# Layer 0 of a two-layer decoder trunk: two of four output-projection groups by seven products

## The chip, the cores and the metric

The kernel runs on one core of a Trainium2 chip. TensorE (PE in the profile) multiplies matrices, with its weight loads shown apart (PEld); VectorE is DVE, ScalarE is ACT, GpSimd is POOL, and SyncE (SP) issues most DMAs. The metric is the device time of one launch in microseconds; lower is better.

## The reference

Two layers (D = 2048, 512 tokens, batch 1), each a modulated mixer with residual. Cut to what matters:

```python
for l in range(DEPTH):                                   # DEPTH = 2
    mod = c_act @ w_mod[l] + b_mod[l]                    # 2048 -> 3 x 2048
    shift, scale, gate = jnp.split(mod, 3, axis=-1)
    h = rmsnorm(x, norm_gain[l]) * (1.0 + scale[:, None, :]) + shift[:, None, :]
    proj = h @ w_in[l]                                   # 2048 -> 7504
    ...  # sparse softmax attention (8 heads) -> y_a, chunked retention (8 heads) -> y_b,
    ...  # each times its own SiLU gate
    y = jnp.concatenate([y_a, y_b], axis=-1) @ w_out[l]  # 2048 -> 2048
    x = x + gate[:, None, :] * y
```

## The kernel before, in words

Everything is held transposed: features on the 128 partitions, 512 tokens along the free axis, so x is 16 tiles of 128x512 float32 (k = 0 to 15). To keep float32 accuracy, each operand of a large product is split into a high part (rounded to fp32r, made on ACT) and a low part (the rest, made on DVE); a product is three matmuls, high-high, high-low and low-high.

The work is one stream of groups. A group is a product with 512 columns of a weight, cut into chunks of two feature tiles, eight chunks in all. A plain chunk takes 2 x 4 x 3 = 24 matmuls with 512 moving columns (`chunk_mm`, L390 to L392, or L396 to L398 where the weights move). Groups of a layer in order: S (keys, values, index), QI or Q3, VB, four QK, two QA, two GA, two GB (all of `w_in`), then four of `w_out`. Attention, retention and other work between products are Python generators (tasks) from which `fill` issues some before each chunk.

`step(i)` issues one chunk: `ahead` loads weights up to four chunks ahead (tile wf, on SP's queue) and splits them two ahead (wh on ACT, wl on DVE; each has three buffers), then the group's `pre`, then modulation, then tasks, then the chunk's matmuls. The order on each engine's queue is set when the program is built, by a scheduler, and is not always that in which the program issues; POOL's order is that of the program.

**Modulation.** `c_act @ w_mod` runs on DVE: `mod_rest` walks the list REST of 64 row tiles (gate of layer 0, shift and scale of layer 1, gate of layer 1), loads each as two halves of 128x1024 (512 KB each, tile mw, two buffers of tag mw, on SP) and `mod_add` (L408) reduces each half against the broadcast vector cb (L417). A tiny POOL copy (L416) holds each reduction behind the newest wl. `MODN` says how many halves a chunk of a group takes, as a running fraction; the last two chunks of layer 0 take none (MX0 = 2). Layer 0 needs the first 96 halves: with the last, `mod_end` (L421) adds the bias and layer 1's shift and scale are ready.

**Output projection.** Layer 0: four plain groups named OUT. `put_y` splits the gated y into high and low (kept in arena tiles HP) while GB's second group runs. `evac_out` (L1461) multiplies by the gate and adds x, which `pre_out` loaded (xr); the new x tile stays in arena tile A(k), its square goes into ssq (`add_sq`), and it is stored to xs for layer 1's residual. The last two chunks are run as two halves of 256 tokens (`out_halves`) so that layer 1's norm (prs, prb) and first h (`make_hh`, L795) start early.

Layer 1: four groups named O7 by seven products. A chunk is a 2x2 block scheme: weights of 256x512 as four blocks of 256 columns and tokens in two halves of 256, seven block products instead of eight. `seven_hi` and `seven_lo` split three blocks of the weights as they are and make four sums (wsum) and split these (ws, in tiles of tag mw, or in pairs of generic tiles); `put_seven` makes and splits four sums of y. Each of the seven products is 2 x 3 matmuls with 256 moving columns: 42 a chunk (L1354 to L1356), into seven PSUM tiles held over the group. `seven_out` combines them on DVE; `seven_put` scales by the gate, POOL adds x from memory in a DMA (`accum_op`, L1398) and POOL stores the result (L1399); the fourth quarter goes by `seven_fin` with x loaded to a tile xr, stored from SP.

Generic tiles (128x512) come from one pool of 28 buffers; PSUM has eight banks under two tags, px (tasks) and pj (groups).

Of the kernel before, what the change touches and what calls it, by code (L numbers as in the profile page):

```python
# [21 lines left out]
P = 128  # L22
# [24 lines left out]
MODN = [{"QA": 0.5, "GA": 1.0, "GB": 1.5, "OUT": 1.65}, {"QK": 0.5, "GA": 1.0}]  # L47
# [89 lines left out]
def hybrid_trunk(ctx, tc, xt, positions, wmod, w_in, w_out, cst_d, dec_d, out):  # L137
# [35 lines left out]
    def f(a):  # L173
        return a.bitcast(F32)
# [79 lines left out]
    st = {"dma": 0, "hi": 0, "split": 0, "i": 0, "mod": 0.0}  # L254
# [11 lines left out]
    def seven_hi(i):  # L266

        if "sum" not in seven:
            seven["sum"] = sm("wsum", D, tag="cb")
        w, s = wf[i], seven["sum"][:, i % 2 * 1024:(i % 2 + 1) * 1024]  # L270
        h = ring.tile([P, 1024], F32R, name="wh", tag="wh")
        act(h[:, :3 * QC], w[:, QC:], AF.Copy)
        tt(s[:, :2 * QC].rearrange("p (b c) -> p b c", c=QC), w[:, :QC].unsqueeze(1).to_broadcast([P, 2, QC]),
           w[:, 2 * QC:].rearrange("p (b c) -> p b c", c=QC), op=OP.subtract)
        tt(s[:, 2 * QC:3 * QC], w[:, 2 * QC:3 * QC], s[:, QC:2 * QC], op=OP.subtract)
        tt(s[:, 3 * QC:], w[:, QC:2 * QC], s[:, 2 * QC:3 * QC], op=OP.subtract)
        if i % 3 < 2:
            t = gen_mw("ws", F32R)
            pieces = [(t[:, :1024], t[:, 1024:], slice(0, 1024))]
        else:  # L280
            pieces = [(G("wsh", F32R), G("wsl", F32R), slice(n * T, (n + 1) * T)) for n in range(2)]
        for sh, _, c in pieces:
            act(sh, s[:, c], AF.Copy)
        whl[i] = h, s, pieces

    def seven_lo(i):
        h, s, pieces = whl[i]
        lo = ring.tile([P, 1024], F32R, name="wl", tag="wl")
        tt(lo[:, :3 * QC], wf.pop(i)[:, QC:], f(h[:, :3 * QC]), op=OP.subtract)
        for sh, sl, c in pieces:  # L290
            tt(sl, s[:, c], f(sh), op=OP.subtract)

        def part(q):
            if q < 3:
                return h[:, q * QC:(q + 1) * QC], lo[:, q * QC:(q + 1) * QC]
            c0 = (q - 3) * QC
            sh, sl, c = next(p for p in pieces if p[2].start <= c0 < p[2].stop)
            o = c0 - c.start
            return sh[:, o:o + QC], sl[:, o:o + QC]
        whl[i] = h, lo, part  # L300
# [50 lines left out]
    def step(budget=3.0, modn=2):  # L351
        i = st["i"]
        st["i"] += 1
        g, ch = stream[i]
        first, last = ch == 0, ch == g.nch - 1
        ahead(i + 5, i + 3)
        if g.pre:
            g.pre(ch)
        st["mod"] += modn
        if whl:  # L360
            state["gate"] = f(whl[max(whl)][1][:, :1])
        while st["mod"] >= 1.0:
            st["mod"] -= 1.0
            next(modgen, None)
# [121 lines left out]


# [32 lines left out]
    def put_seven(p, y0, y1):  # L520
# [24 lines left out]
        put(("T2", "T4"), t24, eh, 0, el, 0)  # L545
        YT[p] = names
# [397 lines left out]
    def layer(l):  # L944
# [386 lines left out]
        def post_seven(ch):  # L1331
            for p in (ch - 1,) if 0 < ch < 7 else (6, 7) if ch == 7 else ():
                put_seven(p, Y.pop(2 * p), Y.pop(2 * p + 1))
# [42 lines left out]
        outv = out.rearrange("(k p) t -> k p t", p=P)  # L1376

        def pre_seven(g):
            def pre(ch):
                if ch == g.nch - 3:  # L1380
# [10 lines left out]
        def seven_put(g, i, t, v):  # L1391
# [7 lines left out]
            (dma if g.end else nc.gpsimd.dma_start)(out=xs_of(outv, g, i, t), in_=halves(v))  # L1399

# [6 lines left out]
        def seven_fin(g, prod, m):  # L1407
# [4 lines left out]
            dma(outv[k][:, t * QC:(t + 1) * QC], r[:, c])  # L1412

# [34 lines left out]
        def pre_out(g):  # L1448
            def pre(ch):
                if ch == 0:  # L1450
                    for n in range(4):
                        t = G("xr")
                        dma(t, xs_d[l][4 * g + n])
                        xr[4 * g + n] = t
            return pre

        def evac_out(g):
            def ev(n, ps):
                k = 4 * g + n
                t = A(k, "xn") if first else G("xo")  # L1460
                stt(t, ps, mod_col(l, 2, k), xr.pop(k), op0=OP.mult, op1=OP.add)  # L1461
                if first:
                    X[k] = t
                    if k == 0:
                        ss["t"] = G("ssq")
                    if k < KT - 4:
                        add_sq(ss["t"], t, k)
                    if k == KT - 5:
                        act(sm("dummy", 1), ss["t"][:, :1], AF.Sqrt)
                    if k < KT - 4:  # L1470
                        dma(xs_d[1][k], t)
                else:
                    dma(out[k * P:(k + 1) * P, :], t)
            return ev

        def out_halves(i):
# [5 lines left out]
            for hf, c in enumerate(HALF):  # L1482
                q = [G("sq") for _ in range(2)]
                for n in range(4):
                    k = KT - 4 + n
                    ps = psum.tile([P, T], F32, name="po", tag=("px", "pj")[hf])[:, :nh]
# [15 lines left out]
                pss, r = PX("prs"), sm("rcol2", 2, bufs=2)  # L1502
# [6 lines left out]
                pb = PX("prb")[:, c]  # L1509
# [9 lines left out]
        S = Group(W_in, [(KA, 256), (KI, 80)], 2, "tok", 4, hact, evac_s, pre=None if first else pre_l1, name="S")  # L1519
# [55 lines left out]
        for g in range(4):  # L1575
            cols = [(QB + 256 * g, 256), (KB + 256 * g, 256)]
            if first and 4 + 2 * g < NE:
                keys = [(4 + 2 * g, 0), (5 + 2 * g, 0), (4 + 2 * g, 1), (5 + 2 * g, 1)]
                seq.append(Group(W_in, cols, 2, "t", 4, hact, joined(keys, evac_qk(g), T), name="QK",
                                 kr=(EARLY[4 + 2 * g], KT)))  # L1580
            else:
                seq.append(Group(W_in, cols, 2, "t", 4, hact, evac_qk(g), name="QK"))
        seq += [Group(W_in, [(QA + 512 * g, 512)], 2, "tok", 4, hact, evac_qa(g), name="QA") for g in range(2)]
        seq += [Group(W_in, [(GA + 512 * g, 512)], 2, "t", 4, hact, evac_g(4 * g), name="GA") for g in range(2)]
        seq += [Group(W_in, [(GB + 512 * g, 512)], 2, "t", 4, hact, evac_g(8 + 4 * g),
                      post=(post_last if first else post_seven) if g == 1 else None, name="GB") for g in range(2)]
# [58 lines left out]
```

## Time and profile before

| | us |
|---|---|
| median of 3 runs | 1850.31 |
| lowest, highest | 1849.68, 1850.46 |
| the profiled execution's own time | 1849.68 |
| its span, first to last instruction | 1847.9 |
| TensorE (PE) busy | 1821.7 |
| VectorE (DVE) busy | 1384.4 |
| ScalarE (ACT) busy | 888.0 |

The mean granted TensorE clock of the execution is 0.994 of full speed. Times in the views are microseconds from the span's start. Approximate places: layer 0's fourth QK group 416 to 469, QA 469 to 571, GA 571 to 696, GB 696 to 783, output groups 783 to 946 and their halves to 960; layer 1's second GB group 1637.6 to 1681.1 and its output groups from 1681.1 on. Rows of instructions read: line, engine, operation, tile written <- tiles read, count, busy time, mean ns of one, and idle time before it with what ended it. In rows of one tile the three numbers are the least, median and greatest ns, then first and last start.

### The profile page before, as it was taken

Reading aid. Unit: us, or ns where it says so; the run is one execution under the profiler, and the core shown is the slowest. Engines: PE = TensorE matmul, PEld = TensorE weight load, DVE = VectorE, ACT = ScalarE, POOL = GpSimd, SP = SyncE. Lnnn points to the kernel's source line nnn. Section 1 sums busy time; section 2 is a strip of 40 time slices with the busy share of each in tenths; the row PEclk is TensorE's granted clock in tenths of the full one; section 3 lists DMA queues with packets and bytes.
Section 4 is the critical chain, followed back from the end, with each engine's and each line's share of the span. In section 5 each row is a group of like instructions: output and inputs, shape, how many; then the busy total and the mean of one; then the engine's idle time right before and its main releaser. Section 6 shows DMA issues by size and latency. Waiting matters only on the chain.

```text
span 1847.9 us, 26300 instructions
## 1 busy us (share of the span) xinstructions
PE 1821.7 (99%) x9644; PEld 1562.9 (85%) x9644; DVE 1384.4 (75%) x2438; ACT 888.0 (48%) x1708; POOL 70.8 (4%) x184
## 2 busy tenths in 40 slices
PE   7999999999999999999999999999999999999998
PEld 7878888888888888888899988888888888889998
DVE  7996699787867846777776699377875686369886
ACT  7668943564546532422235542344444554245443
POOL 0001000000000000100000000000000000000111
PEclk7999999999999999999999999999999999999999
DMA  9995533333454547789864323444534354333554
GB/s 371 364 321 178 165 88 92 109 114 95 123 186 123 174 147 236 233 281 308 304 208 129 103 80 100 142 124 147 155 120 124 93 185 135 102 92 109 149 151 130
DMA packets 175762, 304.55 MB, mean 165 GB/s; under 512 B 16960, under 2 KB 92864, under 8 KB 172048
## 3 DMA queue, kind: packets, MB, share of 16 engines
q1 hardware_dynamic: 171328, 295.23, 50.5%
q0 software_dynamic: 4160, 7.41, 1.6%
q8 instruction: 76, 1.25, 0.3%
q14 instruction: 54, 0.44, 0.1%
q10 hardware_dynamic: 144, 0.22, 0.0%
HBM read 289.18 MB, written 13.63 MB: 164 GB/s over the span
## 4 chain that ended last, share of the span: by engine, by line
PE 83%; DVE 2%; ACT 2%; DMA 1%; issue 1%; SPq 0%; DVEq 0%; ACTq 0%
PE pj L390 15%; PE pj L391 15%; PE pj L392 15%; PE pj L398 6%; PE pj L397 6%; PE pj L396 6%; PE p L1356 3%; PE p L1355 3%; PE p L1354 3%; PE ptr L177 1%; PE pdot L1028 1%; DVE wl L334 1%; PE pdot L1030 1%; ACT wh L324 1%; PE plg L1250 1%
## 5 line engine op out<-in xcount | busy, mean ns | idle before, releaser
L324 ACT ACTIVATE wh<-wf 128x1024 fp32r<-128x1024 f32 (+2 forms) x277 | 284.7, 1029 | 586.9 <-PE pj L391 390.1
L334 DVE TENSOR_TENSOR wl<-wf,wh 128x1024 fp32r<-128x1024 f32 (+2 forms) x277 | 326.6, 1180 | 289.1 <-ACT wh L324 282.5
L390 PE MATMUL pj<-h,wh 128*128 128x512 f32 (+1 forms) x1280 | 488.4, 382 | 1.9 <-ACT bt L911 1.7
L391 PE MATMUL pj<-h,wh 128*128 128x512 f32 (+1 forms) x1280 | 485.9, 380 | 2.6 <-DVE h L631 2.6
L392 PE MATMUL pj<-h,wl 128*128 128x512 f32 (+1 forms) x1280 | 485.7, 379 | 0.5 <-DVE wl L334 0.5
L390 PEld LDWEIGHTS pj<-h,wh 128*128 128x128 f32 x1280 | 240.6, 188 | 44.9 <-issue 2.5
L391 PEld LDWEIGHTS pj<-h,wh 128*128 128x128 f32 x1280 | 240.6, 188 | 42.1 <-DVE h L631 3.8
L392 PEld LDWEIGHTS pj<-h,wl 128*128 128x128 f32 x1280 | 240.5, 188 | 41.4 <-DVE wl L334 1.1
L396 PE MATMUL pj<-wh,h 128*128 128x512 f32 (+1 forms) x616 | 234.6, 381 | 4.1 <-ACT h L625 3.4
L397 PE MATMUL pj<-wl,h 128*128 128x512 f32 (+1 forms) x616 | 233.6, 380 | 0.7 <-DVE wl L334 0.7
L398 PE MATMUL pj<-wh,h 128*128 128x512 f32 (+1 forms) x616 | 232.6, 380 | 0.2 <-DVE h L631 0.2
L396 PEld LDWEIGHTS pj<-wh,h 128*128 128x128 f32 x616 | 116.5, 189 | 26.7 <-ACT h L625 3.9
L397 PEld LDWEIGHTS pj<-wl,h 128*128 128x128 f32 x616 | 116.5, 189 | 20.3 <-DVE wl L334 1.1
L398 PEld LDWEIGHTS pj<-wh,h 128*128 128x128 f32 x616 | 116.2, 189 | 20.4 <-DVE h L631 0.4
L417 DVE CUSTOM_DVE_ANT_0 mw<-mw,cb 128x1024 f32<-128x1024 f32 (+1 forms) x64 | 93.0, 1453 | 7.0 <-POOL mp L416 5.6
L417 DVE CUSTOM_DVE_ANT_0 mw<-mw,cb,mp 128x1024 f32<-128x1024 f32 x68 | 88.3, 1298 | 12.4 <-POOL md L416 7.9
L392 PE MATMUL pj<-y,wl 128*128 128x512 f32 x240 | 93.4, 389 | 0.0
L391 PE MATMUL pj<-y,wh 128*128 128x512 f32 x240 | 93.4, 389 | 0.0
L390 PE MATMUL pj<-y,wh 128*128 128x512 f32 x240 | 93.4, 389 | 0.0
L1262 ACT ACTIVATE bias<-bias,mx 128x128 f32<-128x128 f32 (+1 forms) x64 | 35.9, 561 | 65.3 <-DVE mx L1261 64.6
L1036 DVE SCALAR_TENSOR_TENSOR iacc<-relu,wi,iacc 128x384 f32<-128x384 f32 (+2 forms) x96 | 55.5, 613 | 10.1 <-ACT relu L1034 7.2
L894 ACT ACTIVATE ind<-pos,pt 128x512 bf16<-128x512 f32 (+3 forms) x128 | 61.4, 553 | 0.1
(549 smaller groups left out, 3077.3 us busy)
## 6 DMA issues: line engine op xcount, KB each, us to landing
wf<-in_w_in_dram SPq DMA_DIRECT2D x155, 512.0 KB, 3.7
mw<-in_wmod_dram SPq DMA_DIRECT2D x136, 512.0 KB, 5.7
wf<-in_w_in_dram SPq DMA_DIRECT2D x136, 256.0 KB, 3.1
mw<-in_wmod_dram SPq DMA_DIRECT2D x28, 1024.0 KB, 8.6
wf<-in_w_out_dram SPq DMA_DIRECT2D x32, 512.0 KB, 5.3
wf<-in_w_out_dram SPq DMA_DIRECT2D x64, 256.0 KB, 3.5
dec<-in_decay_dram SPq DMA_DIRECT2D x32, 256.0 KB, 4.0
xT<-in_xt_dram SPq DMA_DIRECT2D x16, 256.0 KB, 5.4
```

The lines of the kernel that those rows point to most:

```text
L324: act(h[:, :n], wf[i][:, :n], AF.Copy)
L334: tt(lo[:, :n], wf.pop(i)[:, :n], f(whl[i][:, :n]), op=OP.subtract)
L390: mm(q, wh[:, o:o + P], ah, start=s0, stop=False)
L391: mm(q, wh[:, o:o + P], al, start=False, stop=False)
L392: mm(q, wl[:, o:o + P], ah, start=False, stop=s1)
L396: mm(q, ah[:, n * P:(n + 1) * P], wh[:, o:o + g.N], start=s0, stop=False)
L397: mm(q, ah[:, n * P:(n + 1) * P], wl[:, o:o + g.N], start=False, stop=False)
L398: mm(q, al[:, n * P:(n + 1) * P], wh[:, o:o + g.N], start=False, stop=s1)
L417: nc.vector.tensor_tensor_reduce(w[:, lo:hi], w[:, lo:hi], cb[:, lo:hi], scale=ng(l, k, 1) if q == 1 else 1.0, scalar=init, op0=OP.mult, o ...
L894: act(v, tab["pos"][:, :w], AF.Sign, bias=tab["pt"][:, col:col + 1], scale=-1.0)
L1036: stt(a[:, :w], r[:, :w], L["WI"][:, c0:c0 + 1], a[:, :w], op0=OP.mult, op1=OP.add)
L1354: mm(dst[m], wh[:, c], bh, start=k == 0 and (own or m == 0), stop=False)
```

## The change

In layer 0 the first two of the four output groups (NW = 2) become O7 groups; the last two stay plain.

- `put_both` makes, per pair of y tiles, the plain split of `put_y` and all four sums (T1 and T3, T2 and T4) split into generic tiles e1, e3 and arena tiles A(2p), A(2p+1). The plain quarters serve as the unsummed factors.
- In layer 0 `seven_hi` writes the weight sums to two generic tiles of 512 columns instead of to cb, which modulation still needs, and splits them in two operations.
- ws takes the buffers of tag mw, so modulation stops at 33 tiles (66 halves, MODSTOP) and resumes (`mod_on`) at the third output group. MODN moves halves to earlier groups and raises the rate of the last two.
- The O7 groups write their part of x (k = 0 to 7) to xs. `squares` (at chunk 2 of the next group) adds their squares to ssq. Since arena tiles A(0) to A(7) held sums of y meanwhile, x of k = 0 to 7 is loaded back from xs during chunks 1 to 4 of the third output group (RELOAD).
- The third output group uses PSUM tag px, the fourth pj. `post_last` is gone; both layers use `post_seven`.

```diff
-MODN = [{"QA": 0.5, "GA": 1.0, "GB": 1.5, "OUT": 1.65}, {"QK": 0.5, "GA": 1.0}]
+NW = 2
+SWAP = NW % 2
+MODN = [{"QK3": 1.0, "QA": 0.75, "GA0": 1.0, "GA1": 2.25, "GB0": 2.5, "OUT": 2.35}, {**{f"QK{g}": 0.5 for g in range(4)}, "GA0": 1.0, "GA1": 1.0}]
+MODSTOP = 33
+RELOAD = {1: (0, 1), 2: (2, 3), 3: (4, 5), 4: (6, 7)}
...
     def seven_hi(i):
-        if "sum" not in seven:
-            seven["sum"] = sm("wsum", D, tag="cb")
-        w, s = wf[i], seven["sum"][:, i % 2 * 1024:(i % 2 + 1) * 1024]
+        w = wf[i]
         h = ring.tile([P, 1024], F32R, name="wh", tag="wh")
         act(h[:, :3 * QC], w[:, QC:], AF.Copy)
...
+            s = [G(f"s{n}") for n in range(2)]
+        tt(s[0].rearrange("p (b c) -> p b c", c=QC), w[:, :QC].unsqueeze(1).to_broadcast([P, 2, QC]),
            w[:, 2 * QC:].rearrange("p (b c) -> p b c", c=QC), op=OP.subtract)
+        tt(s[1][:, :QC], w[:, 2 * QC:3 * QC], s[0][:, QC:], op=OP.subtract)
+        tt(s[1][:, QC:], w[:, QC:2 * QC], s[1][:, :QC], op=OP.subtract)
...
+            if st["modon"] or st["modn"] < 2 * MODSTOP:
+                st["modn"] += 1
...
+                next(modgen, None)
...
+    def mod_on():
+        state["resume"]()
+        st["mod"] = -MODN[0]["OUT"]
...
+    def put_both(p, y0, y1):
+        a, b = slice(0, QC), slice(QC, 2 * QC)
+        t13, t24 = G("t13"), G("t24")
+        tt(t13[:, a], y0[:, b], y0[:, a], op=OP.subtract)
+        tt(t13[:, b], y0[:, b], y1[:, b], op=OP.add)
+        tt(t24[:, a], y1[:, b], t13[:, a], op=OP.add)
+        tt(t24[:, b], y1[:, a], t24[:, a], op=OP.subtract)
+        put_y(2 * p, y0)
+        put_y(2 * p + 1, y1)
...
+        for keys, src, hi, lo in ((("T1", "T3"), t13, G("e1", F32R), G("e3", F32R)),
+                                  (("T2", "T4"), t24, A(2 * p, "eh", F32R), A(2 * p + 1, "el", F32R))):
+            act(hi, src, AF.Copy)
+            tt(lo, src, f(hi), op=OP.subtract)
...
+        def squares():
+            while sq_todo:
+                t, v = sq_todo.popleft()
...
+                    parts = (0, 1)
+                q = G("sq")
+                o = QC * parts[0]
+                act(q[:, o:], v[:, o:], AF.Square)
+                for m in parts:
+                    tt(s, s, q[:, m * QC:(m + 1) * QC], op=OP.add)
...
         def pre_seven(g):
             def pre(ch):
+                if ch == 2:
+                    squares()
...
                         dma(t, xs_d[l][4 * g + n])
                         xr[4 * g + n] = t
+                    if g == NW:
+                        mod_on()
+                if g == NW:
+                    if ch == 2:
+                        squares()
...
+                    for k in RELOAD.get(ch, ()):
+                        X[k] = A(k, "xn")
+                        dma(X[k], xs_d[1][k])
...
+        for n in range(NW if first else 4):
+            g = Group(W_out, [(512 * n, 512)], 2, "7", 4, hact, None, name="O7")
...
         if first:
-            seq += [Group(W_out, [(512 * g, 512)], 2, "t", 4, hact, evac_out(g), pre=pre_out(g), name="OUT")
-                    for g in range(4)]
...
+            seq += [Group(W_out, [(512 * g, 512)], 2, "t", 4, hact, evac_out(g), pool="px", pre=pre_out(g), name="OUT")
+                    for g in range(NW, 3)]
+            seq += [Group(W_out, [(1536, 512)], 2, "t", 4, hact, evac_out(3), pool=("pj", "px")[SWAP], pre=pre_out(3), name="OUT", kr=(0, KT - 4)),
+                    Group(W_out, [(1536, 512)], 2, "t", 4, hact, None, name="OUT", kr=(KT - 4, KT))]
```

More of the change, by code (lines that the diff above doesn't have):

```diff
@@ L266, in seven_hi @@
     def seven_hi(i):
-        if "sum" not in seven:
-            seven["sum"] = sm("wsum", D, tag="cb")
-        w, s = wf[i], seven["sum"][:, i % 2 * 1024:(i % 2 + 1) * 1024]
+        w = wf[i]
         h = ring.tile([P, 1024], F32R, name="wh", tag="wh")
         act(h[:, :3 * QC], w[:, QC:], AF.Copy)
-        tt(s[:, :2 * QC].rearrange("p (b c) -> p b c", c=QC), w[:, :QC].unsqueeze(1).to_broadcast([P, 2, QC]),
+        big = stream[i][0].l == 1
+        if big:
+            if "sum" not in seven:
+                seven["sum"] = sm("wsum", D, tag="cb")
+            o = i % 2 * 1024
+            s = [seven["sum"][:, o + n * T:o + (n + 1) * T] for n in range(2)]
+        else:
+            s = [G(f"s{n}") for n in range(2)]
@@ L286, in seven_lo @@
+        pieces = [(sh, sl, v) for (sh, sl), v in zip(hl, s)]
+        if big and i % 3 < 2:
+            pieces = [(t[:, :1024], t[:, 1024:], seven["sum"][:, o:o + 1024])]
+        for sh, _, v in pieces:
+            act(sh, v, AF.Copy)
+        whl[i] = h, pieces, hl
     def seven_lo(i):
-        h, s, pieces = whl[i]
+        h, pieces, hl = whl[i]
         lo = ring.tile([P, 1024], F32R, name="wl", tag="wl")
         tt(lo[:, :3 * QC], wf.pop(i)[:, QC:], f(h[:, :3 * QC]), op=OP.subtract)
-        for sh, sl, c in pieces:
-            tt(sl, s[:, c], f(sh), op=OP.subtract)
+        for sh, sl, v in pieces:
+            tt(sl, v, f(sh), op=OP.subtract)
@@ L295, in part @@
                 return h[:, q * QC:(q + 1) * QC], lo[:, q * QC:(q + 1) * QC]
[L296 to L299, printed above, removed]
+            o = (q - 3) % 2 * QC
+            return tuple(v[:, o:o + QC] for v in hl[(q - 3) // 2])
         whl[i] = h, lo, part
@@ L472, in load, with resume @@
                 dma(tiles[j][:, lo:lo + D // 2], wmod[2 * KT + j][:, lo:lo + D // 2])
+        def resume():
+            st["modon"] = True
+            for lo in (0, D // 2):
+                load(MODSTOP, lo)
+        state["resume"] = resume
         for j in range(MWBUFS - 1):
@@ L1332, in post_seven @@
             for p in (ch - 1,) if 0 < ch < 7 else (6, 7) if ch == 7 else ():
-                put_seven(p, Y.pop(2 * p), Y.pop(2 * p + 1))
+                (put_both if first else put_seven)(p, Y.pop(2 * p), Y.pop(2 * p + 1))
         def seven_chunk(i):
@@ L1412, in seven_fin @@
             dma(outv[k][:, t * QC:(t + 1) * QC], r[:, c])
+            if first and m:
+                sq_todo.append((t, r))
         def seven_out(g, prod):
@@ L1459, in ev @@
                 k = 4 * g + n
[L1460 to L1467, printed above, removed]
+                X[k] = A(k, "xn")
+                stt(X[k], ps, mod_col(l, 2, k), xr.pop(k), op0=OP.mult, op1=OP.add)
+                if k < KT - 4:
+                    add_sq(ss["t"], X[k], k)
                     if k == KT - 5:
                         act(sm("dummy", 1), ss["t"][:, :1], AF.Sqrt)
[L1470 to L1473, printed above, removed]
+                    dma(xs_d[1][k], X[k])
             return ev
@@ L1518, in layer @@
         gs = []
-        S = Group(W_in, [(KA, 256), (KI, 80)], 2, "tok", 4, hact, evac_s, pre=None if first else pre_l1, name="S")
+        S = Group(W_in, [(KA, 256), (KI, 80)], 2, "tok", 4, hact, evac_s, pool="px" if SWAP and not first else "pj", pre=None if first else pre_l1, name="S")
         part = {}
```

76 lines of the change are left out of this document (43 added, 33 removed).

## The prediction

> **What bounds the kernel now.** I read the page first, then the waits of TensorE, then busy time by stage, then the rows of the two kinds of output projection, and last the queues beside them.
>
> ```profile
> span 1847.9 us, 26300 instructions
> ...
> PE 1821.7 (99%) x9644; PEld 1562.9 (85%) x9644; DVE 1384.4 (75%) x2438; ACT 888.0 (48%) x1708; POOL 70.8 (4%) x184
> ```
>
> ```profile
> PE pvar L1173 <- ACT rsqh L1169: 0.4, 1, 0.4
> PE prb L1511 <- DVE rcol L1508: 0.2, 1, 0.2
> PE patt L1309 <- DVE bias L1258: 0.2, 1, 0.2
> ```
>
> The second fence is every wait of TensorE between 427 and 1000 us (total, times, longest): 0.8 us in 573. So TensorE alone sets the time there; a matmul less is time gained, and another engine costs something only when it makes TensorE wait. Busy time by stage (microseconds and instructions of PE, PEld, DVE, ACT, POOL; then clock, DMA share, GB/s):
>
> ```profile
> 10.00:50.00 40.00, 30.92 (x165) 26.75 (x166) 34.29 (x56) 25.55 (x48) 2.07 (x3) 0.74 1.05 395
> 416.00:469.00 53.00, 52.43 (x248) 44.14 (x248) 41.65 (x54) 26.65 (x46) 0.00 (x0) 1.00 0.31 91
> 643.50:696.00 52.50, 52.50 (x248) 43.78 (x247) 27.16 (x39) 18.41 (x30) 1.88 (x8) 1.00 0.50 160
> 696.00:739.50 43.50, 43.50 (x193) 36.04 (x192) 26.23 (x36) 10.76 (x12) 2.74 (x12) 1.00 0.75 241
> 739.50:783.10 43.60, 43.60 (x194) 36.09 (x194) 34.14 (x49) 17.56 (x26) 6.58 (x12) 1.00 0.73 241
> 870.10:913.70 43.60, 43.60 (x194) 36.07 (x193) 31.18 (x44) 11.03 (x13) 2.46 (x13) 1.00 0.85 294
> ...
> 1637.60:1681.10 43.50, 43.50 (x193) 36.05 (x192) 39.95 (x81) 25.71 (x47) 0.00 (x0) 1.00 0.31 91
> ...
> 1721.50:1761.80 40.30, 40.30 (x338) 40.30 (x338) 32.95 (x52) 18.92 (x29) 5.92 (x6) 1.00 0.59 158
> ```
>
> In order: the start, where the memory queues are fullest; layer 0's fourth QK group, its second GA, first GB and second GB group, its third output group; layer 1's second GB group and its second seven-product output group. In all the late ones PE is full.
>
> **The matmuls (likeliest: minus 6.40 us).** Layer 1 already runs the seven products, so the new price stands in the trace. First starts and last starts of the two forms:
>
> ```profile
> L390 PE MATMUL pj<-y,wh x240: 387/389/398, 783.1 to 945.7; 128*128 128x512 f32 x120
> L392 PE MATMUL pj<-y,wl x240: 389/389/397, 783.5 to 946.1; 128*128 128x512 f32 x120
> L1354 PE MATMUL p<-y,wh x128: 278/283/283, 1681.1 to 1839.2; 128*128 128x256 f32 x128
> L1356 PE MATMUL p<-y,wsl x44: 279/283/283, 1688.6 to 1842.3; 128*128 128x256 f32 x44
> ```
>
> Plain: three lines of 240 are 720 matmuls of 512 columns from 783.1 to 946.1, or 226.7 ns each (163.2/720 with the last one's own share). Seven: 4 groups x 8 chunks x 42 = 1344 of 256 columns from 1681.1 to 1842.3, 120.0 ns each. A chunk is 24 x 226.7 = 5.44 us plain and 42 x 120.0 = 5.04 us by seven products. The arithmetic falls by an eighth, the time by a fourteenth, since a line through the two forms gives 0.417 ns a column and 13.3 ns fixed for each matmul, and there are 42 of them for 24. Sixteen chunks change: 16 x 0.40 = 6.40 us. Rows show no gain elsewhere, as TensorE's other waits there come to 0.8 us; that is the limit of any further gain.
>
> [...]
>
> **Modulation moved ahead.** Halves of 1024 columns, before and after, by groups of layer 0: QK3 0 to 8, each QA 4 to 6, GA0 8 and 8, GA1 8 to 18, GB0 12 to 20, GB1 12 to 0, output groups 13, 13, 13, 10 to 0, 0, 16, 14. Before 97, after 96: one falls to layer 1, where its groups run at half the rate. One chunk of the third output group on VectorE, and the end of layer 0:
>
> ```profile
> 892.98 1.23 DVE L334 TENSOR_TENSOR wl<-wf,wh 128x1024 fp32r<-128x1024 f32 x1 [2.53 <-ACT wh L324]
> 894.49 1.23 DVE L417 CUSTOM_DVE_ANT_0 mw<-mw,cb 128x1024 f32<-128x1024 f32 x1 [0.28 <-POOL mp L416]
> ...
> 895.85 1.28 DVE L417 CUSTOM_DVE_ANT_0 mw<-mw,cb,mp 128x1024 f32<-128x1024 f32 x1
> ...
> 946.17 0.19 DVE L421 TENSOR_TENSOR md<-md,mb 128x32 f32<-128x32 f32 x1
> ...
> 956.41 0.87 DVE L795 SCALAR_TENSOR_TENSOR u<-xn,md,prb 128x256 f32<-128x256 f32 x2 [0.80 <-PE prb L1511]
> ```
>
> A half costs VectorE 1.36 us from start to start (894.49 to 895.85), and the first of a chunk waits 0.28 us for POOL's gate copy. Weights are split two chunks ahead: wl waits for wh, and wh for TensorE to leave a buffer of three.
>
> ```profile
> L324 ACT ACTIVATE wh<-wf 128x1024 fp32r<-128x1024 f32 x8 | 8.5, 1061 | 30.5 <-PE pj L391 30.5
> ```
>
> That row is the third output group's: 30.5 us of ACT's idle time is that buffer. The cover is two chunks less the split, 10.9 - 2.3 = 8.6 us; VectorE may be that late before TensorE stops.
>
> QK3: 41.65 + 8 x 1.64 = 54.8 us in 53: VectorE is full. Between nothing (its tasks are asked for a chunk later) and 2.0 us (the overflow of 1.8 and the wait of 0.4 that already stands at its end, rounded down); I take +0.7, nearer to the tight row. A gain is excluded, nothing is removed there. QA0 and QA1 get two halves each: nothing, by the same cover. GA1: 27.2 + 10 x 1.36 = 40.8 of 52.5, nothing. GB0: 26.2 + 8 x 1.36 = 37.1 of 43.5, nothing, up to +1 if its tiles come late (next part). GB1: minus 12 x 1.36, which nobody waited for.
>
> **GB1 and the entry into seven products.** The halves of y are now made plain and as sums (put_both); layer 1's GB1 does nearly the same with VectorE at 39.95 of 43.5 and no wait of TensorE. +0.2, between nothing and +1, for wsum cut in tiles of 512 and a backlog brought from GB0.
>
> **Squares behind POOL's additions.** Each output half now feeds the sum of squares at chunk 2 of the next group, after POOL has added x by DMA:
>
> ```profile
> 1724.60 1.26 POOL L1398 DMA_DIRECT2D uc<-xs  x1 [138.85 <-ACT uc L1389]
> ...
> 1731.34 1.20 POOL L1398 DMA_DIRECT2D u<-xs  x1 [0.23 <-DMA wf<-in_w_out_dram]
> ...
> 1738.03 1.24 POOL L1398 DMA_DIRECT2D u<-xs  x1
> 1742.80 0.74 POOL L1399 DMA_DIRECT2D out_dram<-u  x1 [3.53 <-DMA u<-xs]
> ```
>
> The group's matmuls ended at about 1721.5; the third addition has landed some 21 us later, in TensorE's chunk 4 of the next group, because POOL keeps addition and store in turn. ACT reaches the squares at about chunk 2 and stands; behind it are the splits of chunk 5, due at 5 x 5.04 = 25.2 us:
>
> ```profile
> L272 ACT ACTIVATE wh<-wf 128x768 fp32r<-128x768 f32 x9 | 7.6, 845 | 17.8 <-PE p L1355 10.7 <-issue 7.1
> L289 DVE TENSOR_TENSOR wl<-wf,wh 128x768 fp32r<-128x768 f32 x8 | 7.6, 954 | 2.5 <-ACT wh L272 2.5
> L556 ACT ACTIVATE sq<-xn 128x512 f32<-128x512 f32 x4 | 2.5, 633 | 2.1 <-DVE xn L1461 2.0
> ```
>
> 21 + 0.63 (square) + 0.85 (wh) + 0.95 (wl) = 23.4: in time by 1.8 us. Landing at 24 it would be late by 1.2, and with the sums' splits behind it by 2.6. I take +0.5, between nothing and 2.6. The work itself is small: four squares of 0.63 on ACT, eight additions of about 0.4 on VectorE (32.95 of 40.3 busy).
>
> **The last two output groups.** Thirty halves in 14 chunks where 23 stood, at 2.35 a chunk: a tile of two halves every 4.63 us. VectorE in the third group: 31.2 + 3 x 1.36 = 35.3 of 43.5, fits. The stream must come through two tile buffers:
>
> ```profile
> mw<-in_wmod_dram SPq DMA_DIRECT2D x24, 512.0 KB, 5.9
> ...
> xr<-in_xt_dram SPq DMA_DIRECT2D x8, 256.0 KB, 5.6
> ```
>
> These are the issues between 870 and 946 us, 5.9 us to landing. A buffer's turn is 5.9 + 2 x 1.36 + 0.28 = 8.9 us, for two buffers 4.45 us a tile: 4% within 4.63. Bytes: 44 transfers of 512 KB (30 halves, 14 chunks) and 20 of 256 KB (8 xr, 8 reloaded x, 4 stores) are 28.3 MB in 14 x 5.44 = 76.2 us, 371 GB/s, against 294 now in the third group and 395 in the row of the start. The reload stands on SP ahead of modulation tiles and waits for POOL's last stores; it holds up the tiles behind it. What hides all this is the end: the last modulation (L421) is done at 946.17 and first used at 956.41, 10.2 us. After the change the last half is the second of its step, 8.9 us. I take +0.7, between nothing and +12 (worked out under the third rival).
>
> [...]
>
> **Sum.** -6.40 + 0.7 + 0.2 + 0.5 + 0.7 = -4.3 us. The profiled execution took 1849.68 us (1.8 of it outside its span of 1847.9), which is the lowest of the three and 0.6 below their median of 1850.31. So 1845.4 against that execution, 1846.0 as a median. About 0.2%, 3.7 us, is what a measurement tells from no change: faster lies below 1846.6.
>
> **Rivals.** *Likeliest: the matmuls' gain stays, small stalls:* 1844 to 1847, 1846.0. For it: layer 1 does the same products with no wait, and 8.6 us of cover. Chance 0.56.
>
> *The gain is mostly spent in new waits of TensorE:* QK3 at its 2.0, the squares at 2.6, 0.5 at GB1 and in the output groups: 1850.3 - 6.4 + 5.1 = 1849.0, no measurable change. For it: VectorE over-full in QK3, ACT standing in order behind POOL. Against: TensorE's waits in the trace are tenths even where VectorE is at 92%. Chance 0.32.
>
> *Slower: the modulation stream ends after layer 1 needs it.* Fifteen tiles follow one another in the last two groups. Above 4.63 + 8.9/15 = 5.2 us a tile the first h of layer 1 waits; from 5.6 (15 x 0.4 = 6 us lost) the whole gain is gone, which is a landing of 8.2 us in place of 5.9. At 6.0, with landings of 9 behind a reload held up by POOL: 15 x 0.8 = 12 us, 1850.3 - 6.4 + 12 = 1855.9. Against: landings at about 294 GB/s were 5.9, and 395 has been moved. Chance 0.10.
>
> *The short matmuls gain more:* without their fixed part both forms cost 0.417 ns a column, a chunk 24 x 213.4 = 5.12 or 42 x 106.7 = 4.48 us, 16 chunks 10.2 us less: 1850.3 - 10.2 + 2.1 = 1842.2. Against: 1344 rows of layer 1 in which the part is paid. Chance 0.02. [...]
>
> **How the numbers follow.** Faster 0.58 (the first with its tail cut, and the last), same 0.32, slower 0.10. Range: from the gain whole, 1850.3 - 6.4 = 1843.9, to 1850.2, which takes in the second rival and leaves out the third and a few hundredths at both ends. The likeliest alone: 1844 to 1847.
>
> **What would show it.** Right: layer 0's first two output groups with 336 matmuls in 40.3 us each; waits of TensorE after 400 us of some 2 us more; L421 within 9 us of the third output group's successor ending. QK3's step is wrong if its waits (pvar, psc, pret) stay at 0.4 or pass 2. The squares' step is wrong if wh or ws of chunks 5 to 7 after a group never ends a wait of PE, or does for over 2.6 us. The stream's step is wrong if mw lands in over 8 us or VectorE waits for mw by more than 5 us in all. The whole is wrong above all if TensorE waits for u or h at the layer's change.

## The result, and the profile after

The changed kernel takes 1868.11 us (median of 5 runs, 1865.72 to 1869.59) against 1850.31 before (1849.68 to 1850.62): ratio 1.0096 [1.0081, 1.0111]. It is slower by some 17.8 us, 1.0%, where 4.3 us less were forecast. Its page begins:

```profile
span 1866.3 us, 27194 instructions
...
PE 1826.3 (98%) x9932; PEld 1576.1 (84%) x9932; DVE 1443.7 (77%) x2583; ACT 916.8 (49%) x1776; POOL 85.9 (5%) x196
```

TensorE's waits between 427 and 1000 us (total, times, longest), 0.8 us in all before:

```profile
PE pj L410 <- DVE wl L348: 4.8, 4, 1.8
PE po L1565 <- ACT wh L338: 2.6, 1, 2.6
PE p L1405 <- DVE wl L305: 2.6, 1, 2.6
PE prs L1579 <- DVE ssq L1573: 1.9, 1, 1.9
PE po L1567 <- DVE wl L348: 0.8, 1, 0.8
```

Each row is of layer 0's output projection: the entry into the seven products (p), the plain groups (pj), the halves of the last two chunks (po, prs). Busy time by stage: QK3, GB1, the two groups by seven products, the 14 plain chunks:

```profile
416.00:469.00 53.00, 52.50 (x248) 44.18 (x248) 48.28 (x66) 26.62 (x45) 4.24 (x7) 1.00 0.51 162
...
739.50:782.50 43.00, 43.00 (x191) 35.63 (x190) 40.70 (x74) 23.02 (x38) 0.00 (x0) 1.00 0.36 120
782.50:868.00 85.50, 82.66 (x673) 82.21 (x673) 71.77 (x128) 44.15 (x76) 5.95 (x6) 0.98 0.52 159
868.00:952.20 84.20, 79.35 (x338) 63.84 (x337) 55.64 (x82) 21.75 (x29) 14.74 (x34) 0.98 0.86 281
```

Up to 782 us nothing is lost. From there, by first starts of TensorE's matmuls in the profiled executions:

| stage, us | before | after | difference |
|---|---|---|---|
| start of layer 0's output projection | 783.1 | 782.5 | -0.5 |
| its first two groups (16 chunks) | 87.0 | 85.5 | -6.4 by the matmuls, +4.8 at the entry |
| the 14 plain chunks | 76.2 | 84.2 | +8.0 |
| the last two chunks, as halves | 13.2 | 22.3 | +9.0 |
| layer 1 up to its output projection | 721.6 | 725.5 | +4.0 |
| layer 1's output projection | 166.8 | 166.3 | -0.5 |

The differences add up to the 18.4 us between the two spans (1866.3 and 1847.9).

Where the 8.0 and 9.0 begin is seen on three engines. POOL first, after the second group's end at 868.0 (start, length, operation, idle time before it and what ended it):

```profile
869.13 1.20 POOL L1470 DMA_DIRECT2D uc<-in_xt_dram  x1 [20.93 <-DVE xr L1478]
877.24 0.75 POOL L1471 DMA_DIRECT2D xs<-uc  x1 [6.92 <-DMA uc<-in_xt_dram]
877.98 1.23 POOL L1470 DMA_DIRECT2D u<-in_xt_dram  x1
882.34 0.74 POOL L1471 DMA_DIRECT2D xs<-u  x1 [3.13 <-DMA u<-in_xt_dram]
883.07 1.25 POOL L1470 DMA_DIRECT2D u<-in_xt_dram  x1
887.94 0.75 POOL L1471 DMA_DIRECT2D xs<-u  x1 [3.62 <-DMA u<-in_xt_dram]
888.68 0.20 POOL L434 COPY mp<-wl 128x1 f32<-128x1 f32 x1
```

Three additions and their stores run in turn for 19.6 us, and modulation's copies (L434) stand behind them in POOL's program order. ScalarE in the same time:

```profile
876.93 0.63 ACT L1444 ACTIVATE sq<-uc 128x512 f32<-128x512 f32 x1 [5.67 <-DMA uc<-in_xt_dram]
877.47 1.04 ACT L338 ACTIVATE wh<-wf 128x1024 fp32r<-128x1024 f32 x1
882.03 0.63 ACT L1444 ACTIVATE sq<-u 128x512 f32<-128x512 f32 x1 [3.52 <-DMA u<-in_xt_dram]
887.38 0.63 ACT L1444 ACTIVATE sq<-u 128x512 f32<-128x512 f32 x1 [4.72 <-DMA u<-in_xt_dram]
887.92 0.62 ACT L1444 ACTIVATE sq<-xr 128x512 f32<-128x512 f32 x1
888.44 2.94 ACT L338 ACTIVATE wh<-wf 128x1024 fp32r<-128x1024 f32 x3
```

The squares wait for the additions, three weight splits behind them; the first of these is chunk 4's, due at 889.8. VectorE stands behind both:

```profile
888.05 0.43 DVE L1446 TENSOR_TENSOR ssq<-ssq,sq 128x256 f32<-128x256 f32 x1 [4.46 <-ACT sq L1444]
888.91 1.28 DVE L435 CUSTOM_DVE_ANT_0 mw<-mw,cb,cst 128x1024 f32<-128x1024 f32 x1 [0.43 <-POOL mp L434]
```

The second row is the first of the 30 halves: 20.9 us after the group began, and the last begins at 964.31, 96.3 after. That is 75.4/29 = 2.60 us a half, 5.2 a tile, so the stream ends some 20 us after the 76.2 us that the 14 chunks took before. VectorE's waits from 868 to 985, the two that matter:

```profile
DVE ssq L1446 <- ACT sq L1444: 13.3, 3, 5.9
DVE mw L435 <- DMA mw<-in_wmod_dram: 12.8, 7, 2.5
```

### The profile page after: what moved, and what is told of

Same layout as the page of the kernel before. It is cut to its first block, busy times and chain, and to the rows that moved or that the text cites. A ratio compares the mean times of both kernels' runs of the same rounds, so it can differ in the third digit from the quotient of the medians.

```text
span 1866.3 us, 27194 instructions
## 1 busy us (share of the span) xinstructions
PE 1826.3 (98%) x9932; PEld 1576.1 (84%) x9932; DVE 1443.7 (77%) x2583; ACT 916.8 (49%) x1776; POOL 85.9 (5%) x196
## 3 DMA queue, kind: packets, MB, share of 16 engines
q1 hardware_dynamic: 175648, 294.18, 48.3%
## 5 line engine op out<-in xcount | busy, mean ns | idle before, releaser
L338 ACT ACTIVATE wh<-wf 128x1024 fp32r<-128x1024 f32 (+2 forms) x261 | 267.3, 1026 | 488.5 <-PE pj L409 255.3
L348 DVE TENSOR_TENSOR wl<-wf,wh 128x1024 fp32r<-128x1024 f32 (+2 forms) x261 | 307.0, 1177 | 213.7 <-ACT wh L338 212.9
L435 DVE CUSTOM_DVE_ANT_0 mw<-mw,cb,cst 128x1024 f32<-128x1024 f32 (+1 forms) x32 | 56.0, 1749 | 16.8 <-DMA mw<-in_wmod_dram 15.7
L277 ACT ACTIVATE wh<-wf 128x768 fp32r<-128x768 f32 x48 | 40.3, 839 | 54.8 <-PE p L1404 33.4
L434 POOL COPY mp<-wl 128x1 f32<-128x1 f32 x64 | 21.8, 340 | 877.5 <-DVE wl L348 877.5
```

The costliest lines, as they stand in the source:

```text
L338: act(h[:, :n], wf[i][:, :n], AF.Copy)
L348: tt(lo[:, :n], wf.pop(i)[:, :n], f(whl[i][:, :n]), op=OP.subtract)
L435: nc.vector.tensor_tensor_reduce(w[:, lo:hi], w[:, lo:hi], cb[:, lo:hi], scale=ng(l, k, 1) if q == 1 else 1.0, scalar=init, op0=OP.mult, o ...
```

## The experiments

One table for all; stages in us from one profiled execution each (the start of the projection varies by 3 us between kernels that are alike up to there, so medians carry the verdicts). The median of before was 1850.3 to 1851.1 beside them.

| | median | ratio [95%] | first two groups | 14 chunks | halves | layer 1 to its projection |
|---|---|---|---|---|---|---|
| before | 1850.3 | | 87.0 | 76.2 | 13.2 | 721.6 |
| after | 1868.1 | 1.0096 [1.0081, 1.0111] | 85.5 | 84.2 | 22.3 | 725.5 |
| e1 no copies on POOL | 1870.6 | 1.0107 [1.0092, 1.0122] | 85.1 | 84.1 | 24.6 | 724.1 |
| e2 additions on VectorE | 1856.1 | 1.0035 [1.0024, 1.0047] | 85.5 | 76.2 | 18.3 | 723.5 |
| e3 squares asked later | 1869.7 | 1.0104 [1.0089, 1.0119] | 85.4 | 85.2 | 20.9 | 725.8 |
| e4 last pairs of y later | 1865.4 | 1.0079 [1.0062, 1.0096] | 81.4 | 85.6 | 22.6 | 724.6 |
| e5 = e2 + e4 | 1853.5 | 1.0015 [1.0005, 1.0024] | 82.8 | 76.2 | 19.8 | 723.4 |
| e6 = e5 + half in VB | 1851.7 | 1.0006 [0.9997, 1.0016] | 81.4 | 76.2 | 18.0 | 722.5 |
| e7 lower rate alone | 1852.6 | 1.0012 [1.0003, 1.0022] | 87.1 | 80.1 | 13.2 | 721.7 |
| e8 = e6 + lower rate | 1847.3 | 0.9984 [0.9975, 0.9993] | 83.5 | 76.2 | 13.2 | 722.6 |
| e9 = e1, reload later | 1870.5 | 1.0106 [1.0091, 1.0122] | 85.5 | 84.7 | 25.4 | 724.3 |
| e10 = e9, squares asked later | 1869.2 | 1.0098 [1.0084, 1.0111] | 87.6 | 80.7 | 26.0 | 723.4 |
| e11 = e5 + lower rate | 1846.9 | 0.9979 [0.9970, 0.9988] | 82.9 | 76.2 | 13.2 | 721.7 |
| e12 no squares | 1866.4 | 1.0082 [1.0064, 1.0100] | 85.7 | 84.6 | 20.9 | 723.9 |
| e13 no squares, no copies | 1870.2 | 1.0098 [1.0080, 1.0117] | 86.9 | 84.0 | 24.5 | 723.5 |
| e14 = e13, reload later | 1862.3 | 1.0065 [1.0048, 1.0082] | 84.5 | 77.2 | 25.3 | 723.9 |

**e1: modulation without POOL's copies** in layer 0's plain groups.

```diff
-        if "gate" in state:
+        if "gate" in state and stream[st["i"] - 1][0].name != "OUT":
```

> The changed kernel, but in layer 0's last two output groups the modulation halves have no gate copy on POOL. Theory P (POOL's queue): the stream started late because its first gate copies (888.7 us) stand in POOL's queue behind three additions and stores of x for the second seven-product group (869 to 888). Without them the first half of the third output group runs before 880 us, the 14 plain chunks take under 80 us (84.2 in the changed kernel, 76.2 by matmuls alone) and the time falls to 1852 to 1860. Rival S (squares): ACT and DVE stand behind the squares that wait for the same additions; with the gate gone the first wl after them is still late, time 1865 to 1869. Rival R (rate): 2.35 halves a chunk do not come through two tile buffers whatever the start; 14 chunks stay at 82 us or more, time above 1863.

1870.6, which fits R alone of the three: the copies alone are not it. The halves begin at once, but SP's queue then stands:

```profile
884.13 0.33 SPq L490 DMA_DIRECT2D mw<-in_wmod_dram  x1
889.42 0.84 SPq L1535 DMA_DIRECT2D xn<-xs  x2
890.31 0.43 SPq L327 DMA_DIRECT2D wf<-in_w_out_dram  x1
890.79 0.94 SPq L490 DMA_DIRECT2D mw<-in_wmod_dram  x2
```

The reload (L1535) waits for POOL's stores, weights and modulation tiles behind it.

**e2: the second group adds x on VectorE**, from tiles loaded by SP and stored by SP; POOL has no DMA there (`sp_add` is true for that group alone).

```diff
-                    for i, t in ((0, 0), (0, 1), (1, 0), (1, 1)) if g.end else ((0, 1),):
+                    for i, t in ((0, 0), (0, 1), (1, 0), (1, 1)) if g.end or sp_add(g) else ((0, 1),):
...
-            if g.end:
+            if g.end or sp_add(g):
                 r = res.pop((i, t))
                 tt(v, v, r, op=OP.add)
```

> The changed kernel, but the second seven-product group of layer 0 adds x on DVE from tiles loaded by SP and stores from SP, so POOL has no DMA after it. Theory P: modulation starts in chunk 1 of the third output group (about 876 us); rival S says the same, as the squares no longer wait either. Both: 14 plain chunks in under 79 us, the halves after them in under 16 us (22.3 in the changed kernel), time 1851 to 1858, with the stall of 2.9 us at the entry of the first seven-product group still there. Rival R (rate): DVE still waits some 20 us in all for mw tiles in these groups, 14 chunks take 82 us or more, time above 1861.

1856.1: at this rate of modulation 12.0 of the 17.8 us hang on POOL's additions. The plain chunks are at 5.44 us each again; the halves, expected under 16 us, take 18.3 and still lose 5.1:

```profile
PE prs L1582 <- DVE ssq L1576: 3.4, 1, 3.4
```

The 14 chunks of e2, and in a second fence the same stage of the kernel before (clock, DMA share and GB/s at the end):

```profile
869.20:945.40 76.20, 76.20 (x339) 63.08 (x338) 61.23 (x91) 23.09 (x30) 7.95 (x30) 1.00 0.96 337
```

```profile
870.10:946.30 76.20, 76.20 (x337) 63.01 (x336) 56.00 (x79) 20.78 (x23) 4.44 (x23) 1.00 0.87 301
```

DMA is nearly always busy here (a share of 0.96). As an estimate, 337 GB/s at a share of 0.96 is 351 for full engines; before, 301/0.87 = 346. At 346 the 28.3 MB of the forecast take 81.8 us, and e2's last half begins 82.3 us after the group's start (951.51), 6 us after TensorE's 14 chunks have ended. That fits a stream bounded by its bytes, but it isn't shown: from 868 to 965 SP also stood 31.4 us until VectorE freed a tile of mw, and no run has a third buffer. Nor is 346 a ceiling: the stage's mean of 337 lies below it, but 12 us of the stage (383 GB/s, shown under e14) and the start (395) lie above.

**e7: a lower rate alone**, additions left on POOL: 10 halves more before the projection, 20 instead of 30 in the last groups.

```diff
-MODN = [{"QK3": 1.0, "QA": 0.75, "GA0": 1.0, "GA1": 2.25, "GB0": 2.5, "OUT": 2.35}, {...}]
-MODSTOP = 33
+MODN = [{"QK2": 1.0, "QK3": 1.0, "QA": 0.875, "GA0": 1.0, "GA1": 2.25, "GB0": 2.5, "OUT": 1.55}, {...}]
+MODSTOP = 38
```

> The changed kernel with the additions on POOL's queue as they are, but modulation moved further ahead: 76 halves before the output projection instead of 66, then 1.55 a chunk instead of 2.35. Hold theory (the stream is held until POOL's additions are over, then has too little time): 20 halves need 31 us at the rate seen in the plain groups, so they end before layer 1 needs them, but squares and the reload stay late: 1856 to 1862. Rival, rate theory (2.35 a chunk is more than DMA and VectorE give in any order): 1850 to 1853. If neither bears: 1866 or more.

1852.6, the rival's number: 15.5 us come back although the first half still begins 21.6 us after the group. (The 31 us of the expectation don't follow from the rows: at the 2.60 us above 20 halves take 52, and here they take 57.8 from the first start to the last.) With e2 this makes a square; loss in the plain chunks and the halves, against 76.2 and 13.2:

| | additions on POOL | additions on VectorE |
|---|---|---|
| 2.35 a chunk | 8.0 + 9.0 (after) | 0 + 5.1 (e2) |
| 1.55 or 1.58 a chunk | 3.9 + 0 (e7) | 0 + 0 (e8, e11) |

Either alone costs 4 or 5 us, both together 17: a late start is dear to a stream that has no slack to catch up.

**e4: the last two pairs of y split later**, in chunks 1 and 2 of the first seven-product group.

```diff
-            for p in (ch - 1,) if 0 < ch < 7 else (6, 7) if ch == 7 else ():
+            for p in (ch - 1,) if 0 < ch < 7 else (6, 7) if ch == 7 and not first else ():
...
+                if first and g.idx == 0 and ch in (1, 2):
+                    put_both(ch + 5, Y.pop(2 * ch + 10), Y.pop(2 * ch + 11))
```

> The changed kernel, but the last two pairs of y tiles (p = 6, 7), which the seven products need in chunks 6 and 7, are split in chunks 1 and 2 of the first seven-product group instead of at the end of GB. Theory: the stall of 2.9 us in chunk 2 (PE waits for wl behind 12 us of put work on DVE), 0.5 more on ws and 1.7 lost at the half clock behind it go, the group takes 40.3 us in place of 45.2, time 1862 to 1865. Rival: DVE is behind from GB on by its modulation, the stall only moves to a chunk or two later; time 1867 to 1870.

1865.4, just above its forecast; the medians gain 2.7 us here and 2.6 from e2 to e5. The first two groups go from 85.5 to 81.4 us, where 16 x 5.04 = 80.6 is all that the matmuls ask; over all runs they take 81.4 to 83.5 us with the later split and 84.5 to 87.6 without. So most of the 4.8 us at the entry was VectorE's backlog from the sums of y.

**e5: both together.**

> The second group's additions on VectorE and the last two pairs of y split two chunks later, together. If the two losses are separate, their gains add: 1856.1 less the 4.1 us that the deferral gave to the seven-product groups, 1852 (1850 to 1854), those groups in 81 to 82 us, the 14 plain chunks in 76.2 and the halves of the last two chunks still late, some 18 us against 13.2. Rival: the deferred sums push VectorE's later work back by as much, and the plain groups or the halves give the gain back: 1855 to 1857.

1853.5, inside the first reading; the entry is a little slower than in e4 (82.8).

**e6 and e8: layer 1's phase, and the rate.** Of the 4.0 us that layer 1 lost before its output projection, about 2.4 lie in its QK groups (204.1 against 201.7, from their first matmul to that of QA) and some 1.4 in its first group. VectorE's waits in the changed kernel from 1215 to 1270 hold this one; the fence after it has TensorE's from 1215 to 1480, the two longest that the kernel before has not:

```profile
DVE s L1183 <- DMA dec<-in_decay_dram: 3.7, 1, 3.7
```

```profile
PE pvar L1222 <- ACT rsqh L1218: 0.9, 2, 0.7
PE psc L1177 <- ACT rh L1147: 0.4, 2, 0.2
```

The load of the decay table (dec) is issued on SP right behind one of modulation's. e6 adds one half in layer 1's VB groups, so that QK begins after 97 halves as before:

```diff
-..., {**{f"QK{g}": 0.5 for g in range(4)}, "GA0": 1.0, "GA1": 1.0}]
+..., {**{f"QK{g}": 0.5 for g in range(4)}, "VB": 0.0625, "GA0": 1.0, "GA1": 1.0}]
```

> As e5, and in layer 1 one half of modulation more in the VB groups, so that layer 1's QK groups begin after 97 halves as before the change, not after 96. In the changed kernel's trace VectorE waits 3.7 us for the decay table in QK, loaded on SP's queue behind a load of mw. If the parity of the halves is what sets that, layer 1 up to its output projection falls from 723.5 to some 721.6 us and the time by 1 to 2 us against e5 (1850 to 1851). Rival: the order of tasks in QK differs for another reason, and the time is that of e5 within 0.5 us.

> As e6, and modulation moved further ahead (76 halves before the output projection, then 1.58 a chunk). What is left late in e6 are the halves of the last two chunks (18 against 13.2 us), whose sums wait for squares on VectorE. If VectorE's load by modulation there is the reason, they come to 13 to 15 us and the time to 1845 to 1847, faster than before by 3 to 5 us. Rival: the squares of the reloaded x and the reload itself are late whatever modulation does: 1849 to 1851; and the moved halves could push QK's groups of layer 0 over VectorE's time: 1852 or more.

e6: layer 1's stage falls by 0.9 us, less than the 1.9 forecast; the medians differ by 1.8, but the two intervals overlap. e8: 1847.3, faster than before by 0.16% (0.07 to 0.25), just above its forecast; the halves are at 13.2, so their lateness was modulation's.

**e11: the lower rate without that half.**

> As e8 without the half in VB, at 1.55 a chunk, so that layer 1's QK groups begin after 96 halves and a fraction of 0.15, as in e7, where layer 1 up to its output projection took 721.7 us (e8: 722.6). If the fraction with which the halves fall among QK's chunks sets those waits, 1845.5 to 1847, below e8 by 0.5 to 1.5 us; if not, 1847 to 1848.5.

1846.9, ratio 0.9979 [0.9970, 0.9988], the fastest version. Layer 1's stage is 721.7, as in e7 and before, and 0.9 below e8. So the parity of the halves alone doesn't set it; where they fall among QK's chunks fits. Added up, the rates ask for QK's first half at chunk 1 here and in e7 (0.15 carried over) and before (0.5 less a rounding error), and at chunk 0 in e6, e8 and after (about 0.55); the first three have 721.6 to 721.7, the others 722.5 to 725.5. These are single executions, and the medians of e8 and e11 don't differ measurably.

**Which queue holds? e3, e9, e10.** e3 asks for the second group's squares at chunk 5 instead of 2; e9 is e1 with the reload at chunks 4 to 7; e10 does all three.

```diff
-                    if ch == 2:
+                    if ch == 5:
                         squares()
```

```diff
-RELOAD = {1: (0, 1), 2: (2, 3), 3: (4, 5), 4: (6, 7)}
+RELOAD = {4: (0, 1), 5: (2, 3), 6: (4, 5), 7: (6, 7)}
```

> The changed kernel, but the squares of the second seven-product group stand at chunk 5 of the third output group, not at chunk 2. Rival S: ACT no longer waits for POOL's additions, the wait of DVE for the squares (19.7 us) goes to under 3, wl of chunks 4 and 5 is in time, time 1856 to 1862. Theory P: the first modulation half still starts at about 888 us, since its gate copy is still behind POOL's stores; time 1864 to 1870.

> The changed kernel, additions on POOL's queue and rate as they are, without POOL's copies for modulation in layer 0's plain groups (as e1), and with x of layer 1 reloaded at chunks 4 to 7 of the third group instead of 1 to 4. In e1 the copies were gone and nothing was gained; there SP's queue stood from 876 to 889 us, with the reload waiting for POOL's stores and the loads of mw behind it. Queue theory (the additions hold the stream through the reload on SP): the first ten halves come at 2.3 us each from the group's start, 14 plain chunks in 77 to 79 us, 1857 to 1861. Rival (the squares on ScalarE and VectorE, which wait for the additions at chunk 2, hold it as much): 1864 to 1869.

> As e9, and the squares of the second seven-product group at chunk 5 instead of 2, so that nothing on any queue waits for POOL's additions before the fifth chunk, while the additions stay where they are. If these three (copies, reload, squares) are all by which the additions hold the stream, the time is that of e2, in which they are off POOL: 14 plain chunks in 76.2 us, 1854 to 1858. If it stays above 1862, the additions cost through something else (their own traffic, the late data itself).

None gained, and e3 seemed to clear the squares. But ScalarE in e3:

```profile
877.87 0.63 ACT L1444 ACTIVATE sq<-uc 128x512 f32<-128x512 f32 x1 [5.90 <-DMA uc<-in_xt_dram]
878.40 1.05 ACT L338 ACTIVATE wh<-wf 128x1024 fp32r<-128x1024 f32 x1
...
888.95 0.63 ACT L1444 ACTIVATE sq<-u 128x512 f32<-128x512 f32 x1 [5.13 <-DMA u<-in_xt_dram]
```

The builder's scheduler kept the squares where they were, ahead of the weight splits, so neither e3 nor e10 tested them. The next runs take them away.

**e12, e13, e14: without those squares** (layer 1's sum of squares lacks the three quarters that POOL's additions finish); e13 also without the copies, e14 also with the later reload.

```diff
-            if first:
+            if first and g.idx < NW - 1:
                 sq_todo.append((t, v))
```

> The changed kernel without the squares of the three quarters that POOL's additions finish in the second seven-product group (they are left out of layer 1's sum of squares); additions, copies for modulation, reload and rate as they are. In e3 and e10 the trace shows that the squares asked for later kept their place on ScalarE's queue: there ScalarE stands 4.9, 3.8 and 6.4 us for the additions with weight splits (wh) behind. ScalarE theory: that stand is what starves TensorE in the third group; without it wh is in time and the group's chunks return to 5.44 us; modulation still begins 20.9 us late by POOL's copies, so the last two chunks stay late: plain chunks 76 to 79 us, 1859 to 1864. Rival (the copies hold as much by themselves): no change, 1866 or more.

> As e12 and without POOL's copies for modulation in layer 0's plain groups (as e1): nothing but the reload waits for POOL's additions. Theory: the additions hold the stream by two things, the squares on ScalarE and the copies on POOL, each of which alone hides the other's removal; then the time is that of e2 (additions on VectorE), 1853 to 1858, with the first halves from the group's start and 14 plain chunks in 76 to 77 us. Rival: the reload on SP's queue behind the stores holds the loads of mw by itself: 1861 or more.

> As e13, and x of layer 1 reloaded at chunks 4 to 7 of the third group, so that no squares on ScalarE, no copies on POOL and no reload on SP wait for POOL's additions before its fifth chunk. In e13 SP's queue stood from 884 to 895 us before the reload and VectorE waited 9.5 us for the loads of mw behind it. Theory: the additions hold the stream through these three queues, each enough by itself; with all three gone the time is that of e2 (additions on VectorE), 1853 to 1859, 14 plain chunks in 76 to 77 us. Rival: even so the additions' own traffic, or the entry of the group, leaves the stream late: 1862 or more.

e12 and e13 gave their rivals' numbers. e12, VectorE: the copies now hold it by themselves.

```profile
892.01 1.28 DVE L435 CUSTOM_DVE_ANT_0 mw<-mw,cb,cst 128x1024 f32<-128x1024 f32 x1 [14.56 <-POOL mp L434]
```

e13, SP's queue and then VectorE: now the reload holds it.

```profile
883.23 0.46 SPq L490 DMA_DIRECT2D mw<-in_wmod_dram  x1
895.17 0.86 SPq L1535 DMA_DIRECT2D xn<-xs  x2
```

```profile
902.92 1.28 DVE L435 CUSTOM_DVE_ANT_0 mw<-mw,cb,mp 128x1024 f32<-128x1024 f32 x1 [9.52 <-DMA mw<-in_wmod_dram]
```

e14: with all three gone the 14 chunks are back at 77.2 us, close to the forecast, but the time, 1862.3, is the rival's, since the halves take 25.3 (e2: 18.3). Part of that is the edit's own cost. The copies hold each reduction behind the newest wl; without them VectorE puts two reductions (945.08 and 946.35) ahead of a weight split whose wh is ready at 944.9, and TensorE waits for it in the halves:

```profile
948.77 0.39 PE L1567 MATMUL po<-y,wl 128*128 128x256 f32 x1 [2.88 <-DVE wl L348]
```

The five runs without the copies (e1, e9, e10, e13, e14) all wait 2.9 to 4.3 us for wl there, and their halves take 24.5 to 26.0 us. Of the four with copies, additions on POOL and 2.35 a chunk (after, e3, e4, e12), none waits more than 0.8 for wl, though 1.4 to 4.1 for wh, and their halves take 20.9 to 22.6. e14's window from 880 to 892, and e2's:

```profile
880.00:892.00 12.00, 12.00 (x54) 9.94 (x54) 6.16 (x8) 2.12 (x2) 3.92 (x4) 1.00 0.97 289
```

```profile
880.00:892.00 12.00, 12.00 (x55) 9.94 (x54) 9.97 (x19) 3.19 (x3) 0.86 (x5) 1.00 1.03 383
```

At nearly the same share (0.97 and 1.03) the engines move 289 GB/s while POOL's additions run, and 383 without them. That the additions hold the stream through several queues is shown for the plain chunks: the squares left alone (e9) or the reload left alone (e13) cost as much as all three. The copies without the reload weren't run. Of e14's 7.0 us over e2 in the halves, 2.9 are the wait above, which e2 with its copies hasn't. At mean granted clocks of 0.990 (e14) and 0.992 (e2), e14 loses 3.8 us more of full clock, some two stretches at half clock (last section), as an estimate from these rounded clocks. Why DMA moves less beside the additions (289 against 383 GB/s) stays open.

## Why the prediction was wrong

- *Matmuls, -6.40:* right. The two groups have chunks of 5.04 us but for one of 9.88; in e4 they take 81.4 us. (That 13.3 ns are a fixed part of each matmul is a line through two forms; weight loads are busy for 82.2 of these groups' 82.7 us of matmuls, and no run tells the two apart. The price doesn't hang on it.)
- *QK3 over-full, +0.7:* nothing was lost; VectorE was busy 48.3 us of 53, not 54.8, since seven of the eight halves fell into the group at 1.26 us of work each, not 1.64, and some 2 us of other work slid out of it. *GA1, GB0:* nothing, as forecast.
- *GB1 and the entry into seven products, +0.2 (0 to 1):* mis-sized; +4.8. VectorE's 40.7 us of 43.0 look like layer 1's 39.95 of 43.5, but the backlog, which was named, was not costed. e4 shows it for most of the 4.8.
- *Squares behind POOL's additions, +0.5 (0 to 2.6):* the third addition landed 19.4 us after the group, near the 21 forecast. What stood behind was wrong: not the split of chunk 5, due at 25.2, but that of chunk 4, due at 21.8, and on VectorE the additions to ssq with everything after them (13.3 us of waiting).
- *The last two output groups, +0.7 (0 to 12):* the step that failed; 8.0 and 9.0 us. Two things. The stream was costed past SP's reload, but not past POOL, where its own copies stand behind three additions: 20.9 us to the first half. And 371 GB/s was held against the start's 395, while the stage moved 337 in e2, where the additions no longer held it; its own row before (294 at 0.85, quoted there) gives an estimate of 346 for full engines. The sign named for this step came: VectorE waited 12.8 us for mw, where 5 were the limit. e2 and e7 show that each of the two, taken away, brings back most of the loss.
- *One half falls to layer 1, at no cost:* layer 1 lost 4.0 us before its output projection, 2.4 of them in QK, where the place of its halves among the chunks fits; no term stood for it.
- *The rivals:* what came is the third's mechanism, the stream ending after layer 1 needs it, at just its 5.2 us a tile; with the late start, and TensorE starved in the plain groups before that, it cost more than the 1855.9 given. TensorE didn't wait for u or h at the layer's change, which was to show it above all (0.3 us), but for weight splits (ScalarE itself waits 6.0 us for weights that SP loads behind modulation's tiles) and for ssq.

With the entry, the additions and the rate put right, e11 ends at 1846.9. That this is near the forecast 1846.0 is in part luck: e11 still loses 2.3 us at the entry (82.9 against 80.6) and nothing in the plain chunks and the halves, while the forecast had 0.2 at the entry and 1.9 elsewhere.

## What to carry to other kernels

Before calling a stage's bytes affordable, hold them against what the same mix of transfers moved in that stage (here 301 GB/s at a share of 0.87), not against the best rate seen elsewhere (395). GB/s over the share is an estimate and no ceiling: 12 us of e2 moved 383. When a step moves, list for every queue what it issues (the tiny copies too) and what stands ahead of each there. When one event releases several queues, taking one wait away shows nothing while another remains; a copy that only orders work may be missed when it goes; and an experiment that asks for a different order must be read in the trace before its time counts.

## What was not expected of the hardware

Between 780 and 980 us the changed kernel's granted clock is at half (0.50) in four stretches of 3.41 us, from 796.74, 905.97, 957.17 and 970.82. Each begins 1.1 to 2.0 us after the end of a wait of TensorE of 1.8 to 2.6 us. The kernel before has a clock of 1.00 from 783.1 to 959.3. TensorE of the changed kernel in the wait of 1.8 us, right after it, in the next 3.4 us, and then:

```profile
902.60:904.70 2.10, 0.34 (x2) 0.00 (x0) 2.10 (x3) 0.00 (x0) 0.00 (x0) 1.00 0.73 224
904.80:906.00 1.20, 1.20 (x5) 1.01 (x6) 1.01 (x1) 1.06 (x1) 0.27 (x2) 0.99 0.81 256
906.00:909.40 3.40, 3.40 (x9) 2.65 (x8) 2.06 (x5) 0.00 (x0) 0.00 (x0) 0.50 0.94 336
909.50:913.00 3.50, 3.50 (x17) 2.85 (x16) 2.98 (x4) 0.00 (x0) 0.30 (x2) 1.00 0.89 315
```

In these stretches matmuls of 512 columns start 427 ns apart instead of 227 (from 906.07), those of 256 columns 213 instead of 120 (from 957.22). As an estimate a stretch so costs 3.41 x (1 - 227/427) = 1.6 or 3.41 x (1 - 120/213) = 1.5 us on top of the wait, and one of the first kind with three of the second some 6.1 of the 17.8 us, contained in the stages above. The full clock between them lasts 105.8, 47.8 and 10.2 us, which is 31, 14 and 3 times 3.41 us: in this execution the changes lie on a grid of 3.41 us. In the interval of that grid just ahead of each stretch TensorE was idle for 1.4 to 2.7 us. In e4 that idle time was no single long wait; one of 1.2 and one of 1.1 us lay in the interval ahead of a stretch:

```profile
886.70:890.11 3.41, 1.06 (x5) 0.39 (x3) 2.98 (x5) 3.30 (x4) 0.99 (x4) 1.00 0.23 81
890.11:893.53 3.42, 3.42 (x8) 2.66 (x9) 3.42 (x8) 0.00 (x0) 1.50 (x2) 0.50 0.77 245
```

Where the limit lies isn't shown: the changed kernel went to half clock after an interval with 1.4 us idle (967.41 to 970.82) and kept the full clock after one with 1.7 (93.60 to 97.01).
